# The head of a fused matmul-GELU-matmul kernel: the first two units as plain products, top rows of x first, W1 tile 1 loaded ahead of the bottom rows

## The chip, the cores and the metric

One Trainium2 chip, one core. The metric is the device time of one execution in microseconds (us). A time is quoted as the median of its runs; the state of every run that is compared below is fast, or "unknown" where a kernel was run only once.

Most of the argument is about tenths of a microsecond in a run of 855 us, which times cannot show: single runs of one kernel spread over 2 us and more. So I use a second measure, the **lead**. From the end of unit 2's period on (23.6 us in the first trace of before; units are explained below) both kernels give PE (TensorE, the matmul engine) the same sequence of matmuls, to the last one. The lead of a run at some moment is the start of one such matmul in the first trace of the kernel before, minus the start of the same matmul in that run. "The lead at 40 us" is taken at the matmul that starts at 40.02 us in the trace of before. A positive lead is time won.

## The reference

```python
batch, m, k, h, n = 16, 512, 768, 3072, 768     # x (16,512,768), w1 (768,3072), b1 (3072), w2 (3072,768)

def reference(x, w1, b1, w2):
    y = np.matmul(x, w1) + b1
    y = 0.5 * y * (1.0 + erf(y / np.sqrt(2.0)))
    return np.matmul(y, w2).astype(np.float32)
```

## The kernel before

The 8192 rows of x are worked off in blocks of 1024. The first product is made in units: a unit is one block times 256 columns of W1 (a "W1 tile"). Rows and columns are split in two, and a unit is computed by seven products of half size instead of eight (a Strassen scheme), each product being 3 matmuls of 128x128 weights and 512 columns. The price is sums of operands on VectorE (DVE): four per W1 tile (`prep_wt`) and four per block of x (`x_sums`).

Units overlap. Period n holds products 1, 5, 6, 2 of unit n and products 7, 3, 4 of unit n-1. ScalarE (ACT) copies between banks of PSUM, the memory that PE writes to, and applies GELU; DVE adds. In these traces an engine does not pass over an operation that has to wait (in run h1 below PE stands still for 3.7 us at a product whose weights have not landed, with other products behind it), which is why the place of an operation in the program matters here.

```python
def prep_wt(n):                     # four sums of one W1 tile, 0.36 us each, queued for DVE
    o = {s: w1_op(wts[n], s) for s in range(7)}
    for d, a, b in ((T3, B22, T1), (T1, T1, B11), (T2, B22, T1), (T4, B21, T2)):
        later(KQ * P, lambda d=d, a=a, b=b: tt(o[d], o[a], o[b], SUB), soon)

def period(i, j, fill):             # i: this unit, j: the one before; cut to the order
    p1(i); copy_xy(i)               # PE, then ACT: bank bX -> bank bY
    p7(j); fill(1); p5(i); fill(2); p3(j); fill(3)
    p6(i)                           # PE accumulates into the bank that copy_xy wrote
    j.right_done(); fill(4)         # ACT: GELU of what DVE added after p3
    p4(j); fill(5); p2(i); fill(6)

def fill_a(pos, slot):              # what is done between the products in period pos; cut
    if pos == at[1, 0] - 2 and slot in (2, 5):          # period 5
        transpose_pe(1, X1_PE[slot // 3])               # next x tiles 3 and 7: PE, then an ACT copy
    if slot == (1 if pos < at[1, 0] else 4) and ...:
        prep_wt(seq[pos + 1][1])                        # the next unit's W1 tile
    if slot == 4 and pos == 3:
        prep_wt(0)
    if slot == 1 and pos in (at[1, 0] - 2, at[1, 0] - 1):
        x_sums(1, soon, ...)                            # half of the next block's x sums each
    ...
```

POOL (GpSimd) issues the loads that convert to half precision; in the traces they land in the order of issue (in that of before x tiles 4 to 7 at 10.8 to 13.7 us, W1 tiles 1 to 3 at 15.7, 17.7 and 19.7 us):

```python
for t in range(4, 8): load_x(0, t)       # x tiles 4..7 (the bottom rows)
for n in range(1, 4): load_wt(n)         # W1 tiles 1, 2, 3
# loads_a(0):
load_wt(4); load_next_x(1, (0, 4, 1, 5)); load_wt(5); load_next_x(1, (2, 6, 3, 7)); load_wt(6)
```

x tiles 0 to 3 and W1 tile 0 come in single precision on the queue of SP (SyncE) and are cast on DVE and ACT. The head then runs unit 0 as eight plain products, because there is no time yet for sums. `spin` issues dummy products that are meant to keep PE's clock up (run h1 below shows the clock after an idle stretch):

```python
nc.vector.tensor_copy(out=w1_raw(wts[0])[:, 0:KQ, :], in_=wf[:, 0:KQ, :])
nc.scalar.copy(out=w1_raw(wts[0])[:, KQ:2 * KQ, :], in_=wf[:, KQ:2 * KQ, :])
...
plain(bX[0], 0, 0, 0)
transpose_pe(0, 4)
plain(bX[0], 0, 0, 1)
transpose_pe(0, 5, nc.vector.tensor_copy)
x_sums(0, soon, top, (0, 1)); flush(soon)
transpose_pe(0, 6)
plain(bY[0], 0, 1, 0)
transpose_pe(0, 7)
x_sums(0, soon, bottom, (0, 1)); flush(soon)
plain(bY[0], 0, 1, 1)
spin(2)
... # the bottom rows of unit 0, then prep_wt(1), the other x sums, and units 1, 2, ... in periods
```

Of the kernel before, what the change touches and what calls it, by code (L numbers as in the profile page):

```python
# [10 lines left out]
P = 128  # L11
ADD = mybir.AluOpType.add
SUB = mybir.AluOpType.subtract
GELU = mybir.ActivationFunctionType.Gelu
# [8 lines left out]
def kernel(  # L23
# [8 lines left out]
    nc = tc.nc  # L32
# [5 lines left out]
    RH = SB // 2  # L38
    nsb = R // SB
    KQ = K // P // 2  # L40
# [56 lines left out]
    Gs = [halves(0), halves(GR)]  # L97
# [20 lines left out]
    def w1_raw(wt):  # L118
        return wt[:, 0:4 * KQ * P].rearrange("p (k c) -> p k c", c=2 * P)

    def w1_op(wt, slot):
        raw = wt[:, 0:4 * KQ * P].rearrange("p (a k b c) -> p a b k c", a=2, k=KQ, b=2)
        if slot in RAW:
            return raw[:, RAW[slot][0], RAW[slot][1]]
        return wt[:, slot * KQ * P:(slot + 1) * KQ * P].rearrange("p (k c) -> p k c", c=P)
# [58 lines left out]
    with tc.manual_schedule():  # L184
# [16 lines left out]
        def flush(q):  # L201
            while q:
                q.pop(0)[1]()
# [20 lines left out]
        def prep_wt(n):  # L224
# [3 lines that stand above are left out]
# [59 lines left out]
        def xh_of(sb, t):  # L287
            if sb < ONE:
                return cut(sb * GR + GR // 2 + t * K, K)
            return xh_late[t % 3]  # L290
# [5 lines left out]
        def xT_of(sb, t):  # L296
            return XTs[sb][:, t // NU, :, (t % NU) * P:(t % NU + 1) * P]

        def transpose_dma(sb, t):
            nc.sync.dma_start_transpose(out=xT_of(sb, t), in_=xhs[t])  # L300

        def transpose_pe(sb, t, copy=nc.scalar.copy):
            for kc in range(2 * KQ):
                nc.tensor.transpose(out=bT[t % 2][:, kc, :], in_=xhs[t][:, kc * P:(kc + 1) * P],
                                    identity=ident[:])
            copy(out=xT_of(sb, t), in_=bT[t % 2][:])

        def blocks(sb):
            XT = XTs[sb]
            return [XT[:, a, c:c + KQ, :] for a in range(2) for c in (0, KQ)]  # L310

        def x_sums(sb, q, r=slice(0, RH), ks=range(4)):
            A11, A12, A21, A22 = [a[:, :, r] for a in blocks(sb)]
            S1, S2, S4 = [a[:, :, r] for a in XSs[sb]]
            n = KQ * len(range(RH)[r])
            ops = ((S1, A21, A22, ADD), (S2, S1, A11, SUB), (A21, A11, A21, SUB), (S4, A12, S2, SUB))
            for k in ks:
                later(n, lambda k=k: tt(*ops[k]), q)
# [400 lines left out]
        make_identity(nc, ident[:])  # L719
        make_identity(nc, idf)  # L720
        nc.gpsimd.tensor_copy(out=xh_of(0, 4)[:, 0:1], in_=xf[:, 0, 0:1])
        for t in range(4, 8):
            load_x(0, t)
        for n in range(1, 4):
            load_wt(n)

        def spin(n):

            for k in range(n):
                nc.tensor.matmul(out=(bX[1], bY[1])[k % 2][:], lhsT=zero[:, 0, 0:P], rhs=zero[:, 0, :],  # L730
                                 start=True, stop=True, skip_group_check=True)

        spin(9)
        for t in range(4):
            xhs[t] = xh_of(0, t)
            nc.vector.tensor_copy(out=xhs[t], in_=xf[:, t, :])
            transpose_pe(0, t)
            if t == 0:
                nc.tensor.transpose(out=bW[:, 0:2 * NH], in_=bf, identity=idf[0:2 * NH, 0:2 * NH])
                nc.scalar.copy(out=b1t[:], in_=bW[:, 0:2 * NH])  # L740
            spin(2)
        nc.vector.tensor_copy(out=w1_raw(wts[0])[:, 0:KQ, :], in_=wf[:, 0:KQ, :])
        nc.scalar.copy(out=w1_raw(wts[0])[:, KQ:2 * KQ, :], in_=wf[:, KQ:2 * KQ, :])

        def plain(dst, row, side, half):
            slot = ((B11, T1), (B21, B22))[half][side]
            for c in range(KQ):
                nc.tensor.matmul(out=dst[:, 0:RH], lhsT=w1_op(wts[0], slot)[:, c, :],
                                 rhs=blocks(0)[2 * row + half][:, c, :],
                                 start=half == 0 and c == 0, stop=half == 1 and c == KQ - 1,  # L750
                                 skip_group_check=True)

        def plain_done(dst, row, side):
            nc.scalar.activation(out=Gs[0][side][:, 0, row, :], in_=dst[:, 0:RH], func=GELU,
                                 bias=b1t[:, side:side + 1])

        top, bottom = slice(0, 2 * P), slice(2 * P, RH)
        plain(bX[0], 0, 0, 0)
        transpose_pe(0, 4)
        plain(bX[0], 0, 0, 1)  # L760
        transpose_pe(0, 5, nc.vector.tensor_copy)
        x_sums(0, soon, top, (0, 1))
        flush(soon)
        transpose_pe(0, 6)
        plain(bY[0], 0, 1, 0)
        transpose_pe(0, 7)
        x_sums(0, soon, bottom, (0, 1))
        flush(soon)
        plain(bY[0], 0, 1, 1)
        spin(2)  # L770
        for row, banks in enumerate(((bX[0], bY[0]), (bW, bZ))):
            for side in range(2):
                if row:
                    plain(banks[side], row, side, 0)
                    plain(banks[side], row, side, 1)
                plain_done(banks[side], row, side)
        prep_wt(1)
        last = [soon.pop()]
        for k in (2, 3):
            for r in (top, bottom):  # L780
# [19 lines left out]
        def loads_a(pos):  # L800
            if pos == 0:
                load_wt(4)
                load_next_x(1, (0, 4, 1, 5))
                load_wt(5)
                load_next_x(1, (2, 6, 3, 7))
                load_wt(6)
            for n in range(7, NH):
                if pos == at[1, over[n]] + 1:
                    load_wt(n)
            if pos in w2_at_pos:  # L810
                load_w2(*w2_at_pos[pos])

        X1_PE = (3, 7)

        def fill_a(pos, slot):
            if pos == at[1, 0] - 2 and slot in (2, 5):
                transpose_pe(1, X1_PE[slot // 3])
            if slot == (1 if pos < at[1, 0] else 4) and pos + 1 < len(seq) and seq[pos + 1][0] == 0:
                prep_wt(seq[pos + 1][1])
            if slot == 4:  # L820
                if pos == 3:
                    prep_wt(0)
                for m, c in ((21, 9), (22, 0), (23, 3), (23, 6)):
                    if pos == m:
                        prep_w2(T2, c, queue)
                        prep_w2(T3, c, late if m == 23 else queue)
                if pos == 23:
                    for c in range(0, NH, W2C):
                        prep_w2(T4, c, late)
            if slot == 1:  # L830
                if pos in (at[1, 0] - 2, at[1, 0] - 1):
                    h = pos - at[1, 0] + 2
                    x_sums(1, soon, slice(h * RH // 2, (h + 1) * RH // 2))
                if pos == at[0, NH - 1] + 2:
                    for c in range(0, NH, W2C):
                        prep_w2(T1, c, queue)
                    for k in (0, 1):
                        g_sum(k, 0)
            if pos > at[0, NH - 1]:
                if slot in (1, 4):  # L840
                    sums((0, 1100, 0, 0, 1500)[slot])
            elif slot in (1, 2, 4, 5):
                sums((0, 600, 300, 0, 600, 300)[slot])
            if slot == 5:
                loads_a(pos)
                if 1 <= pos < 5:
                    for t in (pos - 1, pos + 3):
                        if t not in X1_PE:
                            transpose_dma(1, t)
                if seq[pos][0] == 1:  # L850
                    keep(seq[pos][1])
            if slot == 6:
                flush(soon)
# [184 lines left out]
            units += [(Unit3, sb, k) for k in range(7)]  # L1038
        prev = None
        for g, (kind, sb, k) in enumerate(units):  # L1040
            if g == 0:
                loads_a(0)
                continue
            cur = kind(g, sb, k)
            if g < len(seq):
                period(cur, prev, lambda slot: fill_a(g, slot))
            else:
                f = {Unit1: fill_mm1, Unit2: fill_lean if sb else fill_mm2_one, UnitH: fill_hyb,
                     Unit3: fill_mm2_two}[kind]
                period(cur, prev, lambda slot: f(sb, k, slot))  # L1050
            prev = cur
# [30 lines left out]
```

## Time and profile before

| | before |
|---|---|
| time, median of the 3 runs there were | 855.16 us (854.98 to 856.19) |
| span of the profiled run | 854.0 us |
| PE busy | 845.9 us, 99% |
| first useful product | 9.93 us |
| unit 3's first product | 25.1 us |

From the page of the kernel before: each engine's busy time and share of the span, PE's busy tenths in 40 slices of the span, and the chain of waits that ended last.

```profile
PE 845.9 (99%) x6407; PEld 566.5 (66%) x6407; DVE 667.5 (78%) x1128; ACT 423.9 (50%) x688; POOL 83.7 (10%) x135
...
PE   8999999999999999999999999999999999999998
...
PE 96%; DMA 3%; POOL 0%; issue 0%; DVE 0%
```

PE is the limit nearly everywhere; only the first and the last slice have room, and the change is about the first. The timeline of the head shows that room (lines picked out of it). Columns: start, duration, engine, line, operation, output<-inputs and shape, count, and in brackets the idle time of the engine before it with what ended it.

```profile
7.92 0.56 DVE L736 CAST arena<-arena 128x768 f16<-128x768 f32 x1 [0.84 <-DMA arena<-in_x_dram]
9.08 0.80 ACT L306 COPY arena<-bT 128x768 f16<-128x768 f16 x1 [0.45 <-PE bT L304]
9.93 0.81 PE L748 MATMUL bX<-arena 128*128 128x512 f16 x3 [0.46 <-ACT arena L306]
10.96 0.49 PE L304 MATMUL bT<-ident,arena 128*128 128x128 f16 x6 [0.22 <-DMA arena<-in_x_dram]
17.81 0.81 PE L379 MATMUL bX<-arena 128*128 128x512 f16 x3
24.46 1.46 PE L379 MATMUL bX<-arena 128*128 128x512 f16 x6
```

L736 is the cast of x tile 3, L306 the copy of its transpose, L748 the plain products, L304 the transpose of an x tile as it lands, L379 the products of the seven-product units. Between 9.93 and 17.81 us PE has 24 matmuls to do (5.2 us) and four transposes (1.4 us), 6.6 us of work in 7.9. The six matmuls at 24.46 are product 2 of unit 2 and product 1 of unit 3, which starts at 25.1.

L189 is DVE's sums (here the preparation of W1 tile 6), L632 and L395 an addition and the GELU that waits for it, L597 `copy_xy`, and the six matmuls at 41.96 begin with product 6 of unit 6, which needs that copy:

```profile
36.34 1.14 DVE L189 TENSOR_TENSOR arena<-arena 128x384 f16<-128x384 f16 x3
37.39 0.68 DVE L632 TENSOR_TENSOR arena<-bZ,arena 128x512 f32<-128x512 f32 x1
38.11 1.15 ACT L395 ACTIVATE arena<-arena,b1t 128x1024 f16<-128x1024 f32 x1 [0.26 <-DVE arena L632]
40.02 0.81 PE L379 MATMUL bY<-arena 128*128 128x512 f16 x3
41.00 0.60 ACT L597 COPY bY<-bX 128x512 f32<-128x512 f32 x1
41.96 1.46 PE L379 MATMUL bY<-arena 128*128 128x512 f16 x6
```

The copy ends at 41.60 and PE starts at 41.96 without having waited: some 0.3 us are to spare (0.36, less some 0.05 for handing over, as in the trace of after below).

### The profile page before, as it was taken

The numbers are of one execution on the slowest core, as the hardware profiler recorded it, in microseconds if no ns is written. First come the engines' busy times: TensorE is split into PE (matmuls) and PEld (weight loads), VectorE is DVE, ScalarE is ACT, GpSimd is POOL, SyncE is SP. The second block draws the span as 40 slices with busy tenths as digits, with TensorE's granted clock in tenths as the row PEclk, the third lists the DMA queues.
The fourth block names the chain that finished last, engine by engine and source line by source line (L and its number), as shares of the span: only waits on it lengthen the run. The fifth ranks groups of instructions, "written<-read, shape, count | busy, mean of one in ns | idle before, by whom it ended". The sixth has DMA issues, their size and how long they took to land.

```text
span 854.0 us, 16428 instructions
## 1 busy us (share of the span) xinstructions
PE 845.9 (99%) x6407; PEld 566.5 (66%) x6407; DVE 667.5 (78%) x1128; ACT 423.9 (50%) x688; POOL 83.7 (10%) x135
## 2 busy tenths in 40 slices
PE   8999999999999999999999999999999999999998
PEld 4444445687544897448974499645995469944798
DVE  5856678786657998669976799667996689957997
ACT  5777762122277513874138722477216771267611
POOL 5021100002100002000020000200012000010000
PEclk9999999999999999999999999999999999999999
DMA  9996987659989698996989889897998969967397
GB/s 226 235 232 89 256 165 269 240 194 216 234 225 291 212 321 293 265 287 228 333 287 271 254 275 334 274 339 158 313 347 264 307 170 333 348 218 266 101 304 286
DMA packets 143522, 219.05 MB, mean 256 GB/s; under 512 B 61756, under 2 KB 84724, under 8 KB 143444
## 3 DMA queue, kind: packets, MB, share of 16 engines
q1 hardware_dynamic: 117968, 179.83, 65.7%
q0 software_dynamic: 25440, 38.15, 21.1%
q8 instruction: 50, 0.82, 0.4%
q14 instruction: 28, 0.23, 0.1%
q10 hardware_dynamic: 36, 0.01, 0.0%
HBM read 180.30 MB, written 47.87 MB: 267 GB/s over the span
## 4 chain that ended last, share of the span: by engine, by line
PE 96%; DMA 3%; POOL 0%; issue 0%; DVE 0%
PE bY L379 21%; PE bY L484 15%; PE bX L379 14%; PE bX L484 10%; PE bZ L379 7%; PE bW L379 7%; PE bZ L484 5%; PE bW L484 5%; PE bY L423 5%; DMA arena<-w1s 2%; PE bZ L423 2%; PE bX L423 2%; PE bW L423 2%; DMA arena<-in_x_dram 1%; PE bY L571 1%; PE bX L571 1%
## 5 line engine op out<-in xcount | busy, mean ns | idle before, releaser
L189 DVE TENSOR_TENSOR arena<-arena 128x1536 f16<-128x1536 f16 (+7 forms) x632 | 403.5, 669 | 6.5 <-PE bW L423 1.1
L379 PEld LDWEIGHTS <-arena 128*128 128x128 f16 x1995 | 194.2, 98 | 229.6 <-DMA arena<-w1s 3.9
L484 PEld LDWEIGHTS <-arena 128*128 128x128 f16 x3528 | 292.1, 98 | 8.3 <-issue 0.3
L379 PE MATMUL bY<-arena 128*128 128x512 f16 x855 | 216.7, 379 | 0.0
L604 DVE TENSOR_TENSOR arena<-bY,arena 128x512 f32<-128x512 f32 (+1 forms) x103 | 70.1, 680 | 130.1 <-PE bY L379 89.6
L379 PE MATMUL bX<-arena 128*128 128x512 f16 x570 | 140.4, 379 | 1.5 <-DMA arena<-w1s 1.5
L597 ACT COPY bY<-bX 128x512 f32<-128x512 f32 (+1 forms) x144 | 79.2, 550 | 120.7 <-DVE arena L533 87.3
L484 PE MATMUL bY<-arena 128*128 128x192 f16 x1500 | 138.3, 246 | 0.0
L395 ACT ACTIVATE arena<-arena,b1t 128x1024 f16<-128x1024 f32 x95 | 109.2, 1149 | 54.8 <-DVE arena L632 54.8
L617 ACT COPY arena<-bW 128x512 f32<-128x512 f32 (+1 forms) x148 | 81.6, 552 | 91.5 <-PE bW L484 43.5
L484 PE MATMUL bX<-arena 128*128 128x192 f16 x1020 | 93.1, 246 | 0.0
L632 DVE TENSOR_TENSOR arena<-bZ,arena 128x512 f32<-128x512 f32 (+1 forms) x103 | 70.0, 679 | 22.8 <-PE bZ L379 18.8
L379 PE MATMUL bZ<-arena 128*128 128x512 f16 x285 | 77.0, 379 | 0.0
L379 PE MATMUL bW<-arena 128*128 128x512 f16 x285 | 77.0, 379 | 0.0
L423 PEld LDWEIGHTS <-arena 128*128 128x128 f16 x528 | 51.6, 98 | 34.1 <-issue 0.2
L400 ACT ACTIVATE arena<-bX,b1t 128x512 f16<-128x512 f32 x95 | 64.7, 681 | 10.4 <-PE bX L379 10.3
L516 POOL DMA_DIRECT2D out_dram<-arena x42 | 30.6, 728 | 395.1 <-DVE arena L628 358.6
L400 ACT ACTIVATE arena<-bY,b1t 128x512 f16<-128x512 f32 x95 | 64.0, 674 | 0.0
L648 ACT COPY bZ<-bY 128x512 f32<-128x512 f32 (+1 forms) x54 | 29.0, 537 | 65.5 <-DVE arena L632 30.5
L294 POOL DMA_DIRECT2D arena<-in_x_dram x60 | 32.5, 546 | 260.9 <-DMA arena<-arena 152.9
L650 DVE COPY bZ<-bY 128x512 f32<-128x512 f32 (+1 forms) x63 | 43.5, 691 | 6.3 <-DVE arena L632 0.5
L484 PE MATMUL bZ<-arena 128*128 128x192 f16 x504 | 48.5, 246 | 0.0
(60 smaller groups left out, 392.3 us busy)
## 6 DMA issues: line engine op xcount, KB each, us to landing
arena<-w2s SPq DMA_DIRECT2D x294, 288.0 KB, 4.7
arena<-w1s SPq DMA_DIRECT2D x72, 672.0 KB, 6.4
out_dram<-arena POOLq DMA_DIRECT2D x42, 384.0 KB, 5.4
w2s<-arena SPq DMA_DIRECT2D x49, 288.0 KB, 3.1
arena<-in_x_dram POOLq DMA_DIRECT2D x60, 192.0 KB, 6.8
w1s<-arena SPq DMA_DIRECT2D x12, 672.0 KB, 8.1
arena<-in_w_dram POOLq DMA_DIRECT2D x17, 384.0 KB, 8.5
out_dram<-arena SPq DMA_DIRECT2D x17, 384.0 KB, 3.4
```

What stands on the lines that cost most here:

```text
L189: nc.vector.tensor_tensor(out=o, in0=a, in1=b, op=op)
L294: nc.gpsimd.dma_start(out=xhs[t], in_=xr[:, sb * 8 + t, :])
L379: nc.tensor.matmul(out=dst[:, 0:RH], lhsT=w1_op(self.wt, slot)[:, c, :], rhs=a[:, c, :], start=first and c == 0, stop=c == self.C - 1, ski ...
L395: nc.scalar.activation(out=self.G[1][:, hi, :, :], in_=self.tmp, func=GELU, bias=b1t[:, 2 * hi + 1:2 * hi + 2])
L400: nc.scalar.activation(out=self.G[0][:, hi, row, :], in_=bank[:, 0:RH], func=GELU, bias=b1t[:, 2 * hi:2 * hi + 1])
L423: nc.tensor.matmul(out=dst[:, 0:N2], lhsT=a, rhs=w[:, :, c, :], start=first and c == 0, stop=c == self.C - 1, skip_group_check=True)
L484: nc.tensor.matmul(out=dst[:, t * N4:(t + 1) * N4], lhsT=a, rhs=w[:, c, :], start=first and c == 0 and t == ts[0], stop=c == NQ - 1, skip_ ...
L597: nc.scalar.copy(out=bY[u.g % 2][:, 0:u.F], in_=bX[u.g % 2][:, 0:u.F])
L604: nc.vector.tensor_tensor(out=u.c22(), in0=bY[u.g % 2][:, 0:u.F], in1=w[:, 0:u.F], op=ADD)
L617: nc.scalar.copy(out=w[:, 0:u.F], in_=bW[:, 0:u.F])
L632: nc.vector.tensor_tensor(out=u.c12(), in0=bZ[:, 0:u.F], in1=w[:, 0:u.F], op=ADD)
L650: nc.vector.tensor_copy(out=bZ[:, 0:u.F], in_=bY[u.g % 2][:, 0:u.F])
```

## The change

The intent: give PE something to do while the bottom rows of x arrive. Unit 1 becomes a plain unit too, W1 tile 1 is loaded ahead of x tiles 4 to 7, and the top rows of both units are computed first. The remaining bottom rows follow in pieces of 256 columns. The last piece of unit 1 sits inside unit 2's period. The sums of W1 tile 1, which unit 1 no longer needs, are made in period 4 for its use with the next block. The first pieces are made smaller so that PE starts earlier.

```diff
         nc.gpsimd.tensor_copy(out=xh_of(0, 4)[:, 0:1], in_=xf[:, 0, 0:1])
+        load_wt(1)
         for t in range(4, 8):
             load_x(0, t)
-        for n in range(1, 4):
+        for n in range(2, 4):
             load_wt(n)
 ...
-            transpose_pe(0, t)
+            transpose_pe(0, t, copy_halves if t == 3 else nc.scalar.copy)
 ...
-        nc.vector.tensor_copy(out=w1_raw(wts[0])[:, 0:KQ, :], in_=wf[:, 0:KQ, :])
-        nc.scalar.copy(out=w1_raw(wts[0])[:, KQ:2 * KQ, :], in_=wf[:, KQ:2 * KQ, :])
+        for r, c in ((slice(0, KQ), slice(0, P)), (slice(0, KQ), slice(P, 2 * P)),
+                     (slice(KQ, 2 * KQ), slice(0, 2 * P))):
+            nc.vector.tensor_copy(out=w1_raw(wts[0])[:, r, c], in_=wf[:, r, c])
 ... (plain and plain_done take the unit, and a range of rows)
+        for half in range(2):
+            for side in range(2):
+                plain(0, 0, side, half)
+        for side in range(2):
+            plain_done(0, 0, side)
+        plain(1, 0, 0, 0)
         transpose_pe(0, 4)
+        plain(1, 0, 0, 1)
+        plain_done(1, 0, 0)
         transpose_pe(0, 5, nc.vector.tensor_copy)
+        plain(1, 0, 1, 0)
+        transpose_pe(0, 6)
+        plain(1, 0, 1, 1)
+        plain_done(1, 0, 1)
+        plain(0, 1, 0, 0, top)
+        plain(0, 1, 1, 0, top)
+        transpose_pe(0, 7, nc.vector.tensor_copy)
 ... (the other top pieces, the x sums, the bottom pieces; no dummy products)
-        prep_wt(1)
+        prep_wt(2)
 ...
+            if pos == 2 and slot == 1:
+                plain(1, 1, 1, 1, bottom)
+                plain_done(1, 1, 1)
             if slot == 4:
-                if pos == 3:
-                    prep_wt(0)
+                if pos in (3, 4):
+                    prep_wt(pos - 3)
```

More of the change, by code (lines that the diff above doesn't have):

```diff
@@ L300, in transpose_dma, with copy_halves @@
             nc.sync.dma_start_transpose(out=xT_of(sb, t), in_=xhs[t])
+        def copy_halves(out, in_):
+            for c in (slice(0, KQ), slice(KQ, 2 * KQ)):
+                nc.scalar.copy(out=out[:, c, :], in_=in_[:, c, :])
         def transpose_pe(sb, t, copy=nc.scalar.copy):
@@ L741 @@
             spin(2)
-        nc.vector.tensor_copy(out=w1_raw(wts[0])[:, 0:KQ, :], in_=wf[:, 0:KQ, :])
-        nc.scalar.copy(out=w1_raw(wts[0])[:, KQ:2 * KQ, :], in_=wf[:, KQ:2 * KQ, :])
-        def plain(dst, row, side, half):
+        for r, c in ((slice(0, KQ), slice(0, P)), (slice(0, KQ), slice(P, 2 * P)),
+                     (slice(KQ, 2 * KQ), slice(0, 2 * P))):
+            nc.vector.tensor_copy(out=w1_raw(wts[0])[:, r, c], in_=wf[:, r, c])
+        banks = {(0, 0): (bX[0], bY[0]), (1, 0): (bX[1], bY[1]),
+                 (0, 1): (bW, bZ), (1, 1): (bX[1], bY[1])}
@@ L746, in plain @@
+        def plain(n, row, side, half, r=slice(0, RH)):
             slot = ((B11, T1), (B21, B22))[half][side]
             for c in range(KQ):
-                nc.tensor.matmul(out=dst[:, 0:RH], lhsT=w1_op(wts[0], slot)[:, c, :],
-                                 rhs=blocks(0)[2 * row + half][:, c, :],
-                                 start=half == 0 and c == 0, stop=half == 1 and c == KQ - 1,
-                                 skip_group_check=True)
-        def plain_done(dst, row, side):
-            nc.scalar.activation(out=Gs[0][side][:, 0, row, :], in_=dst[:, 0:RH], func=GELU,
-                                 bias=b1t[:, side:side + 1])
@@ L757, with plain_done @@
-        top, bottom = slice(0, 2 * P), slice(2 * P, RH)
-        plain(bX[0], 0, 0, 0)
+                nc.tensor.matmul(out=banks[n, row][side][:, r], lhsT=w1_op(wts[n], slot)[:, c, :],
+                                 rhs=blocks(0)[2 * row + half][:, c, r],
+                                 start=half == 0 and c == 0 and r.start == 0,
+                                 stop=half == 1 and c == KQ - 1, skip_group_check=True)
+        def plain_done(n, row, side):
+            nc.scalar.activation(out=Gs[0][side][:, n, row, :], in_=banks[n, row][side][:, 0:RH],
+                                 func=GELU, bias=b1t[:, 2 * n + side:2 * n + side + 1])
@@ L759 @@
+        top, bottom = slice(0, 2 * P), slice(2 * P, RH)
+        for half in range(2):
[4 more added lines that the diff above has]
+        plain(1, 0, 0, 0)
         transpose_pe(0, 4)
-        plain(bX[0], 0, 0, 1)
+        plain(1, 0, 0, 1)
+        plain_done(1, 0, 0)
         transpose_pe(0, 5, nc.vector.tensor_copy)
+        plain(1, 0, 1, 0)
+        transpose_pe(0, 6)
+        plain(1, 0, 1, 1)
@@ L762 @@
+        plain_done(1, 0, 1)
+        plain(0, 1, 0, 0, top)
+        plain(0, 1, 1, 0, top)
+        transpose_pe(0, 7, nc.vector.tensor_copy)
+        plain(0, 1, 0, 1, top)
+        plain(0, 1, 1, 1, top)
+        for side in range(2):
+            for half in range(2):
+                plain(1, 1, side, half, top)
         x_sums(0, soon, top, (0, 1))
-        flush(soon)
-        transpose_pe(0, 6)
-        plain(bY[0], 0, 1, 0)
-        transpose_pe(0, 7)
         x_sums(0, soon, bottom, (0, 1))
@@ L768 @@
         flush(soon)
-        plain(bY[0], 0, 1, 1)
-        spin(2)
-        for row, banks in enumerate(((bX[0], bY[0]), (bW, bZ))):
-            for side in range(2):
-                if row:
-                    plain(banks[side], row, side, 0)
-                    plain(banks[side], row, side, 1)
-                plain_done(banks[side], row, side)
-        prep_wt(1)
+        for side in range(2):
+            for half in range(2):
+                plain(0, 1, side, half, bottom)
+            plain_done(0, 1, side)
@@ L778 @@
+        plain(1, 1, 0, 0, bottom)
+        plain(1, 1, 0, 1, bottom)
+        plain_done(1, 1, 0)
+        plain(1, 1, 1, 0, bottom)
+        prep_wt(2)
         last = [soon.pop()]
@@ L813, with transposes_a @@
         X1_PE = (3, 7)
+        def transposes_a(pos):
+            for t in (pos - 1, pos + 3):
+                if t not in X1_PE:
+                    transpose_dma(1, t)
         def fill_a(pos, slot):
+            if pos == 2 and slot == 1:
+                plain(1, 1, 1, 1, bottom)
+                plain_done(1, 1, 1)
             if pos == at[1, 0] - 2 and slot in (2, 5):
@@ L845, in fill_a @@
                 loads_a(pos)
-                if 1 <= pos < 5:
-                    for t in (pos - 1, pos + 3):
-                        if t not in X1_PE:
-                            transpose_dma(1, t)
+                if pos < 5:
+                    transposes_a(pos)
                 if seq[pos][0] == 1:
@@ L1040 @@
         for g, (kind, sb, k) in enumerate(units):
-            if g == 0:
-                loads_a(0)
+            if g < 2:
+                loads_a(g)
+                if g:
+                    transposes_a(g)
                 continue
```

## The prediction

> **What bounds it now.** PE: busy 845.9 of 854.0 us (page, part 1), 96% of the chain of waits (part 4). The change touches only the first 25 us; what it saves should survive, as everything later follows PE's pace.
>
> **The head now (timeline).** x tiles 0 to 3 are cast at 4.01, 5.45, 6.40, 7.92 us, the first half of W1 tile 0 at 9.00. The first product starts at 9.93, after waiting 0.5 us for ACT's 0.80 us copy of x tile 3. The chain runs through x tiles 4 to 7, transposed as they land (10.96, 11.94, 12.81, 13.81); unit 0 ends at 17.8, unit 3 starts at about 25.1. From 9.93 to 17.8, 24 matmuls at 0.216 us (six start in 1.29) are 5.2, four transposes of 0.34 are 1.4: about 1.3 us are gaps and dummy products. Another 0.17 is lost at 19.1.
>
> **What the change does.**
> - Unit 1 as 8 plain products instead of 7: three more matmuls, +0.65 us.
> - PE has W1 tile 1 and the top rows to work on while the bottom rows arrive: up to 1.3 us, and the 0.17, can go.
> - x tile 3 is copied in halves (estimate 0.45 us each, from 0.80), W1 tile 0 cast in DVE pieces of about 0.3, 0.3, 0.56 us (0.56 measured for 768 columns): first product at 9.6, -0.3.
> - 36 matmuls of 256 columns replace 18 of 512. The Trainium skill (TensorE: Matmul & The Clock Gate, "Back-to-back issue gap") gives N/2.4 + 2.5 ns, 109 ns; its 216 for 512 agrees with this trace. +0.05, at most +0.2.
> - Loads: same bytes, other order. The Trainium skill (DMA: Bandwidth & Descriptors, "Issuing engines are not separate DMA queues") has all queues on the same 16 engines. Read from when POOL's waits end, a W1 tile takes 2.0 us, an x tile 0.95. Estimate: W1 tile 1 lands at 11.9 instead of 15.9, x tiles 4 to 7 at 12.9, 13.85, 14.8, 15.85; W1 tiles 2 and 3 unchanged (17.9, 20).
>
> **Sum on the chain.** First product 9.6; 15 matmuls to 12.85; tile 4 at about 12.95 (gap 0.1 to 0.4); then 33 matmuls' worth (7.1), transposes (1.4), 0.15 for the small matmuls: both units complete at 21.7, counting the 0.33 us piece inside unit 2's period. Unit 2 needs 2.6 us: unit 3 starts at 24.35 against 25.1. Gain about 0.75 us.
>
> DVE is the risk: x sums start after tile 7's copy (17.6) and end at about 23.2; PE needs the first at 22.1, the last at 25. Preparing tile 1 moves to period 4, so periods 3 and 4 carry about 5.0 us of DVE work in 4.53; I estimate DVE 1.5 us behind, within the 2 us before PE waits.
>
> **Prediction: 854.4 us**, 8 in 10 between 853.6 and 855.4. Faster by over 2%: 0.5%; within: 99%; slower: 0.5%.
>
> **What would show it.** First product near 9.6; W1 tile 1's first near 12.2; tile 4's transpose near 13 after a gap under 0.5; no dummy product after 9.5; unit 3's first product near 24.35; no PE wait on DVE between 21 and 45 us; then 4.53 us periods and a span shorter by 0.75.
>
> **What would make it wrong.** W1 tile 1 landing after 12.5, interleaved with x tile 3 and W1 tile 0, pushing all x tiles. DVE so late that it holds PE. A later DMA wait (W1 rereads near 260 and 372 us) absorbing the shift.

## The result, and the profile after

| | before | after |
|---|---|---|
| time, median | 855.0 us (854.53 to 856.19, 6 runs) | 854.96 us (853.71 to 856.6, 6 runs) |
| span of the profiled run | 854.0 us | 852.4 us |
| first useful product | 9.93 us | 10.02 us |
| unit 3's first product | 25.1 us | 24.4 us |
| lead at 40, 43, 50 us | | 0.73, 0.18, 0.09 us |

The ratio is 0.9999, with a 95% interval of 0.9986 to 1.0012. A ratio is the mean time of one kernel's fast runs over that of the other's of the same rounds, so it is not quite the ratio of the medians above. No change of the time is to be seen. The page of the changed kernel, the same lines:

```profile
PE 845.8 (99%) x6432; PEld 569.2 (67%) x6432; DVE 667.8 (78%) x1128; ACT 421.1 (49%) x686; POOL 83.3 (10%) x135
...
PE   9999999999999999999999999999999999999998
...
PE 93%; DMA 5%; ACT 1%; DVE 0%; issue 0%; POOL 0%; ACTq 0%
```

The head, lines that answer to those of before (L741 is now the cast of x tile 3, L304 the half copies, L757 the plain products, L308 the transposes, L383 the units):

```profile
8.05 0.83 DVE L741 CAST arena<-arena 128x768 f16<-128x768 f32 x1 [0.53 <-DMA arena<-in_x_dram]
9.49 0.86 ACT L304 COPY arena<-bT 128x384 f16<-128x384 f16 x2 [0.56 <-PE bT L308]
10.02 0.81 PE L757 MATMUL bX<-arena 128*128 128x512 f16 x3
...
12.62 0.81 PE L757 MATMUL bX<-arena 128*128 128x512 f16 x3
13.27 0.50 PE L308 MATMUL bT<-ident,arena 128*128 128x128 f16 x6
...
23.73 1.46 PE L383 MATMUL bX<-arena 128*128 128x512 f16 x6
```

From 10.02 us PE works without a gap. W1 tile 1 is there when it is needed (12.62), and x tile 4 as well (13.27). The loads landed as estimated: W1 tile 1 at 12.0 us (11.9 predicted), x tiles 4 to 7 at 13.0, 14.0, 14.9 and 15.8 (12.9 to 15.85), W1 tiles 2 and 3 at 17.8 and 19.9 (17.9 and 20). Six matmuls of 256 columns start in 0.65 us, so one takes the predicted 0.109. Unit 3 starts at 24.4 instead of 25.1, so the lead is 0.73 us, and I had summed it up to 0.75. Twenty microseconds later most of it is gone:

```profile
36.47 1.14 DVE L189 TENSOR_TENSOR arena<-arena 128x384 f16<-128x384 f16 x3 [0.32 <-DMA arena<-in_w_dram]
37.53 0.68 DVE L636 TENSOR_TENSOR arena<-bZ,arena 128x512 f32<-128x512 f32 x1
38.24 1.15 ACT L399 ACTIVATE arena<-arena,b1t 128x1024 f16<-128x1024 f32 x1 [1.12 <-DVE arena L636]
39.29 0.81 PE L383 MATMUL bY<-arena 128*128 128x512 f16 x3
41.13 0.60 ACT L601 COPY bY<-bX 128x512 f32<-128x512 f32 x1
41.78 1.46 PE L383 MATMUL bY<-arena 128*128 128x512 f16 x6 [0.38 <-ACT bY L601]
```

Read it upwards. PE waits at 41.78 for `copy_xy` on ACT. ACT reaches that copy late because its GELU (38.24) waited 1.12 us for DVE's addition (L636). DVE was late because the preparation of W1 tile 6 stands ahead of that addition, and waited 0.32 us for that tile's load. In both kernels this string of work stands at nearly the same absolute time (36.34 and 36.47 us), though PE before it was 0.73 us earlier. The chain of waits of the two kernels up to 46 us says the same. Before, from 12.8 us on it is PE (but for 0.01 us):

```profile
36.27 0.34 PE bT L304 x6
36.61 0.65 PE bZ L379 x3
```

After (start, duration, what), it leaves PE at 41.78 and goes back through ACT and DVE into the stream of loads, and does not come back to PE:

```profile
13.26 11.10 DMA arena<-in_x_dram
24.35 0.28 issue
24.64 11.81 DMA arena<-in_w_dram
36.44 0.02 issue
36.47 0.37 DVE arena L189
...
41.78 1.46 PE bY L383 x6
```

The loads are what did not move. By the traces' packet records POOL's queue starts at 8.7 us in both kernels and keeps step in both, whatever the order: as many bytes as everything up to and including W1 tile 5 makes (3456 KB) are through at 26.9 us before and 27.0 after, and those of all x tiles ahead of W1 tile 6 at 31.5 in both. The last packet of W1 tile 6 is in at 35.6 and 36.0, and its semaphore is complete at 35.99 and 36.44. Run h1 below adds that this landing does not follow PE: there PE was 5 us late, and the tile landed at 35.99.

**A trap.** The profiled spans differ by 1.6 us, and the profiled runs' times by as much (855.75 and 854.13). This is not the change. The lead is 0.09 us from 50 to 255 us, and then jumps: 0.67 at 300, 0.29 at 380, 1.2 at 392 us. The first jump is a delay in the first trace of before itself: all 13 other traces, b2_before's too, gain 0.47 to 0.59 us on it between 255 and 300 us. The jumps lie where PE waits for W1 tiles that are read back (`w1s`). The two traces, and the second trace of the unaltered kernel before (label b2_before, told below), differ there:

```profile
PE bX L379 <- DMA arena<-w1s: 1.5, 3, 1.2
```

```profile
PE bX L383 <- DMA arena<-w1s: 0.5, 1, 0.5
```

```profile
PE bX L379 <- DMA arena<-w1s: 6.7, 4, 2.7
```

That is: total us waited, times, longest, for before, after, and before again. The last of them took 861.33 us with no change at all.

### The profile page after: what moved, and what is told of

Its sections match the earlier page's. It is cut to its first block, busy times and chain, and to the rows that moved or that the text cites. A ratio compares the mean times of both kernels' runs of the same rounds, so it can differ in the third digit from the quotient of the medians.

```text
span 852.4 us, 16481 instructions
## 1 busy us (share of the span) xinstructions
PE 845.8 (99%) x6432; PEld 569.2 (67%) x6432; DVE 667.8 (78%) x1128; ACT 421.1 (49%) x686; POOL 83.3 (10%) x135
## 4 chain that ended last, share of the span: by engine, by line
PE 93%; DMA 5%; ACT 1%; DVE 0%; issue 0%; POOL 0%; ACTq 0%
PE bY L383 20%; PE bY L488 15%; PE bX L383 13%; PE bX L488 10%; PE bZ L383 7%; PE bW L383 7%; PE bZ L488 5%; PE bW L488 5%; PE bY L427 5%; DMA arena<-in_x_dram 3%; PE bZ L427 2%; PE bW L427 2%; PE bX L427 2%; DMA arena<-in_w_dram 1%; DMA arena<-w1s 1%; PE bY L575 1%
## 5 line engine op out<-in xcount | busy, mean ns | idle before, releaser
L383 PEld LDWEIGHTS <-arena 128*128 128x128 f16 x1974 | 192.4, 98 | 225.7 <-DMA arena<-w1s 1.8
L383 PE MATMUL bY<-arena 128*128 128x512 f16 x846 | 214.4, 379 | 0.4 <-ACT bY L601 0.4
L383 PE MATMUL bX<-arena 128*128 128x512 f16 x564 | 138.6, 379 | 0.6 <-DMA arena<-w1s 0.5
L636 DVE TENSOR_TENSOR arena<-bZ,arena 128x512 f32<-128x512 f32 (+1 forms) x102 | 69.3, 679 | 22.7 <-PE bZ L383 18.7
L383 PE MATMUL bZ<-arena 128*128 128x512 f16 x282 | 76.2, 379 | 0.0
L383 PE MATMUL bW<-arena 128*128 128x512 f16 x282 | 76.2, 379 | 0.0
L488 PE MATMUL bW<-arena 128*128 128x192 f16 x504 | 48.5, 246 | 0.0
```

The source lines that it names most:

```text
L383: nc.tensor.matmul(out=dst[:, 0:RH], lhsT=w1_op(self.wt, slot)[:, c, :], rhs=a[:, c, :], start=first and c == 0, stop=c == self.C - 1, ski ...
L488: nc.tensor.matmul(out=dst[:, t * N4:(t + 1) * N4], lhsT=a, rhs=w[:, c, :], start=first and c == 0 and t == ts[0], stop=c == NQ - 1, skip_ ...
L636: nc.vector.tensor_tensor(out=u.c12(), in0=bZ[:, 0:u.F], in1=w[:, 0:u.F], op=ADD)
```

## The experiments

Theory **L** (loads): PE's pace near 42 us hangs on a load that lands at a time fixed by the queue, so an earlier PE only waits longer. Rival **D**: DVE has fallen behind because the change put the preparation of W1 tile 1 into period 4. Rival **A**: ACT's own work is too long there. A further rival is that the loss is chance, as the later jumps are.

All outputs are right. The table collects what the texts below use. "Start" is when DVE begins to prepare W1 tile 6. In the changed kernel PE's product at 41.78 starts 5.31 us after it, and its counterpart in before starts at 41.96; so, if that string of work holds PE, the lead behind it is 41.96 - 5.31 - start = 36.65 - start.

| run | lead at 40 us | start | 36.65 - start | lead at 43 us | lead at 50 us |
|---|---|---|---|---|---|
| after (first trace) | 0.73 | 36.47 | 0.18 | 0.18 | 0.09 |
| n1_after | 0.92 | 36.26 | 0.39 | 0.38 | 0.30 |
| e1_prep1_later | 0.59 | 36.03 | 0.62 | 0.59 | 0.52 |
| e2_w6_early | 0.38 | 36.00 | 0.65 | 0.38 | -0.11 |
| e4_three_dummies | 0.75 | 36.05 | 0.60 | 0.60 | 0.49 |
| h1_w1_behind_x | -5.05 | 41.84 | -5.19 | -5.19 | -5.27 |
| h2_whole_copies | 0.14 | 36.66 | -0.01 | 0.00 | -0.50 |
| e5_pool_later | 1.12 | 36.19 | 0.46 | 0.46 | 0.37 |
| b2_before | -0.14 | 36.63 | 0.02 | -0.14 | -0.14 |
| e6_w6_late | -0.23 | 37.44 | -0.79 | -0.80 | -0.88 |
| v1_prep1_later_keeps | 0.75 | 36.37 | 0.28 | 0.27 | 0.19 |
| e3_x_transposes_early | 1.02 | 36.40 | (chain altered) | 0.41 | -0.18 |
| v5_all | 0.97 | 36.45 | (chain altered) | -0.26 | -0.73 |

In every row that keeps the string of work as it is, the lead at 43 us is the smaller of the lead at 40 us and 36.65 - start, within 0.03 us. The 5.31 comes from the first row, so the other rows test it. They test the string of work, whatever sets its start: DVE waited for tile 6's load before it in after, n1, e1, e5, e6 and v1 (0.20 to 0.70 us; 0.06 in b2), and came to it later than the load in e2, e4, h1 and h2.

### n1_after: the changed kernel again

No edit.

> The changed kernel again, unaltered. In the first pair of traces the same product on PE starts 0.73 us earlier than in the kernel before from about 24 us on (the lead), the lead falls to 0.18 at 42 us and to 0.09 at 46 us, and later moves by up to 1 us at the reloads of W1 near 260 to 390 us. If the fall at 42 us is a property of the schedule, it repeats within 0.1 us; if it is chance like the later ones, the lead at 50 us lands anywhere from 0 to 0.7. Time: within 0.1% of before either way.

Measured: 855.04 us (853.95 to 855.83) against 855.04 us of before, ratio 0.9999 (0.9985 to 1.0014). The lead was 0.92, 0.38 and 0.30 us at 40, 43 and 50 us. The fall repeats (0.54 us against 0.55), so it is not chance. The lead itself varies with the first landings, and widely: the seven runs with the head of the changed kernel (after, n1, e1, e2, e3, e6, v1) have leads of -0.23 to 1.21 us at 30 us. Their median is 0.75.

### b2_before: the kernel before again

No edit.

> The kernel before, again, to see how far its own first 25 us move from run to run. Its leads against its first trace should be within 0.3 us of 0 from 24 to 255 us, with no fall at 42 us; after 260 us they may move by 1 us.

Measured: the lead is -0.14 us all the way from 24 to 255 us. There is no fall at 42 us. After 260 us it loses 5 us to reloads of W1 (the third wait line above), far more than the 1 us I had allowed. So in the head a difference under 0.2 us means nothing (and larger ones between single runs little, see n1), and the reloads decide a single run's time.

### e1_prep1_later: tile 1 prepared in period 7

```diff
-                if pos in (3, 4):
-                    prep_wt(pos - 3)
+                if pos == 3:
+                    prep_wt(0)
 ...
+            if pos == at[1, 0] and slot == 1:
+                prep_wt(1)
```

> The preparation of W1 tile 1 (4 DVE operations, 1.46 us) moved from period 4 to period 7. Theory D (DVE is behind because of this preparation): the lead at 50 us comes back to 0.5 or more. Theory L (DVE waits for W1 tile 6, whose landing did not move): DVE is free earlier but still waits for tile 6 until about 36.4 us, its wait there grows from 0.32 us to over 1 us, and the lead at 50 us stays within 0.1 of 0.09.

Measured: one run, 862.28 us. The lead stayed: 0.59, 0.59, 0.52. Taken alone this speaks for D, and against L as I had put it. But tile 6 happened to be usable at 36.03 us in this run, 0.2 to 0.4 earlier than in the two runs of the changed kernel, and then L too has nothing to take away. The run could not tell them apart. It also had a cost of its own: PE waited 6.2 us for W1 tile 7 near 57 us, because write-backs of W1 tiles, queued behind that of tile 1, had moved to 48 to 54 us and met that load. The rest of the 8.6 us that the lead lost there goes with a granted clock of 0.55 from 60.5 to 66 us.

### v1_prep1_later_keeps: the same without the jam

```diff
 (on top of e1)
-                if seq[pos][0] == 1:
+                if seq[pos][0] == 1 and seq[pos][1] not in range(1, 7):
                     keep(seq[pos][1])
+                if pos == at[1, 1]:
+                    for k in range(2, 7):
+                        keep(k)
 ... (keep(1) just before the loads of period 9)
```

> e1 again (tile 1 prepared in period 7), with the write-backs of W1 tiles 2 to 6 queued ahead of that of tile 1, which waits for its preparation. In e1 they stood behind it, ran 10 us later and met the load of W1 tile 7. Expected: no 6.2 us wait of PE near 57 us; the lead at 43 us is the smaller of the lead at 40 us and 36.65 minus DVE's start on tile 6; at 50 us it is within 0.1 of that and it is still there at 100 us: 0.2 to 0.7.

Measured: one run, 853.75 us; no wait for W1 tile 7; lead 0.75, 0.27, 0.19. This time the tile was late, and DVE, with nothing of tile 1 to do, waited longer for it:

```profile
34.98 0.69 DVE L608 TENSOR_TENSOR arena<-bY,arena 128x512 f32<-128x512 f32 x1 [0.90 <-PE bY L383]
36.37 1.15 DVE L189 TENSOR_TENSOR arena<-arena 128x384 f16<-128x384 f16 x3 [0.70 <-DMA arena<-in_w_dram]
```

DVE was free 0.7 us before tile 6 and PE waited 0.32 us for ACT at 41.69 us: the lead still fell to what the start of that preparation allows. D alone is out as the cause. It keeps a part: in the changed kernel DVE is free only at about 36.1 us (its addition at 35.47 takes 0.68), so even an instant load would have left no more than 36.65 - 36.1, about 0.5 us.

### e6_w6_late: one more load ahead of W1 tile 6

```diff
                 load_next_x(1, (2, 6, 3, 7))
+                nc.gpsimd.dma_start(out=cut(o_w2, K), in_=xr[:, 8, :])
                 load_wt(6)
```

> The changed kernel with one more load of an x tile (192 KB, never read) queued just ahead of W1 tile 6. Theory L in numbers: the lead after 42 us is 36.65 minus the time at which DVE starts to prepare W1 tile 6. The extra load takes 1.0 to 1.4 us there, so DVE starts at 37.3 to 37.7, its wait for the load grows to about 1.5 us, and the lead at 43 us is -0.6 to -1.1, from about 0.8 at 40 us. If the landing is not what holds PE (only the amount of DVE and ACT work is), the lead at 43 us stays at 0.2 to 0.6.

Measured: one run, 857.91 us. DVE started at 37.44 us and the lead at 43 us was -0.80, against -0.79 from the rule. Its wait for the load was 0.33 us and not 1.5, because in this run the head was slow (lead -0.23 at 40 us instead of the 0.8 I had assumed; PE waited 1.3 us for a cast of x) and DVE came later as well. So the run shows that PE follows the start, and the start the landing, but it is a smaller step than intended.

### e4_three_dummies: 0.65 us of PE work added to the head

```diff
         transpose_pe(0, 7, nc.vector.tensor_copy)
 ...
+        spin(3)
         for side in range(2):
             for half in range(2):
                 plain(1, 1, side, half, top)
```

> Three dummy products of 0.216 us added to the head (0.65 us of PE work) behind the top rows of x. If the lead is lost because the work at 36 to 42 us hangs on loads that land at a fixed time (L, and D in so far as it hangs on the landing of x tile 7): the lead at 40 us is 0.08, and at 50 us it is 0.0 to 0.1, so 0.65 us of extra work costs under 0.1 us. If it is lost to something that follows PE's own pace: the lead at 50 us falls to about -0.55.

Measured: one run, 853.97 us; lead 0.75, 0.60, 0.49. The dummies ran (17.19 to 17.84 us), but the first landings were early by chance: the first product started at 9.30 us instead of 10.02. So the lead at 40 us was not 0.08, and the test of "extra work is free" was not made. What stands is that even with the addition the lead at 50 us is 0.49 us, among the largest, which fits a limit set by the loads but does not prove it. No wait for tile 6 was recorded; DVE itself was free only at 36.05.

### e2_w6_early: W1 tile 6 loaded ahead of the next x tiles 3 and 7

```diff
-                load_next_x(1, (2, 6, 3, 7))
-                load_wt(6)
+                load_next_x(1, (2, 6))
+                load_wt(6)
+                load_next_x(1, (3, 7))
```

> W1 tile 6 is loaded ahead of the next x tiles 3 and 7 instead of behind them; nothing else. Theory L: no DVE wait on W1 tile 6 near 36.4 us (0.32 us before), the DVE and ACT work behind it moves up by 0.3, and the lead at 50 us is 0.4 to 0.7. Theory D: the lead at 50 us stays at 0.1 to 0.2. Theory A (ACT is the limit, with the copy of x tile 7 among its work there): 0.1 to 0.2 as well.

Measured: one run, 854.28 us; lead 0.38, 0.38, -0.11. DVE's wait for tile 6 was gone and it started at 36.00, as L says. But the lead did not survive: x tiles 3 and 7 now came late, PE lost 0.4 us at its transpose of tile 3 at 35.7 us, and DVE waited 0.5 us at 39.3 us for x tiles transposed by the DMA engines. The expected 0.4 to 0.7 was wrong: moving one load forward moves others back, and they are needed just as soon.

### e3_x_transposes_early: ACT's copy of x tile 7 out of the way

```diff
-            if pos == at[1, 0] - 2 and slot in (2, 5):
-                transpose_pe(1, X1_PE[slot // 3])
+            if (pos, slot) in ((at[1, 0] - 3, 5), (at[1, 0] - 2, 2)):
+                transpose_pe(1, X1_PE[pos - at[1, 0] + 3])
```

> The two PE transposes of the next x tiles 3 and 7 each one place earlier (end of period 4 and early in period 5), so that ACT's 0.8 us copy of tile 7 no longer stands between its GELU and the copy that PE waits for at 42 us. In four traces that wait ended 5.31 us after DVE began the preparation of W1 tile 6 (36.0 to 36.5 us). If that chain through ACT is what takes the lead away, it becomes 0.5 to 0.8 us shorter, PE does not wait there, and the lead at 50 us is within 0.15 of the lead at 40 us, so 0.6 to 0.9. If DVE alone is the limit, the lead falls at 42 us by 0.4 or more as before. Time: 0.5 us shorter than before at best, under 0.1%, so the interval will hold 1 either way.

Measured: 854.58 us (853.6 to 855.25) against 854.75 of before, ratio 0.9993 (0.9978 to 1.0008). PE no longer waited for ACT. It waited for DVE instead, 0.4 us for its next addition and 0.4 us for its next copy, and the lead went 1.02, 0.41, -0.18:

```profile
36.40 1.15 DVE L189 TENSOR_TENSOR arena<-arena 128x384 f16<-128x384 f16 x3 [0.73 <-DMA arena<-in_w_dram]
39.45 2.09 DVE L189 TENSOR_TENSOR arena<-arena 128x768 f16<-128x768 f16 x4 [0.25 <-DMA arena<-arena]
41.46 0.68 DVE L608 TENSOR_TENSOR arena<-bY,arena 128x512 f32<-128x512 f32 x1
```

Theory A alone is out as the cause: with ACT's part 0.8 us shorter the loss was larger, as the next wait, on DVE (0.38 us), stood just behind it. DVE waits for loads twice here (tile 6, then the DMA transposes), and its queue behind them is full.

### h1_w1_behind_x: the old order of loads

```diff
-        load_wt(1)
         for t in range(4, 8):
             load_x(0, t)
-        for n in range(2, 4):
+        for n in range(1, 4):
```

> The changed kernel with the old order of loads: W1 tile 1 behind x tiles 4 to 7. The products of unit 1 then stand in PE's order ahead of x tile 4 but their weights land near 15.5 us. Expected: PE waits about 2.5 to 3 us from about 12.6 us, unit 3's first product about 2 us later than in the changed kernel, lead at 40 us between -1 and -2. If the order of loads did not matter, the lead would stay at 0.7 to 0.9.

Measured: one run, 859.46 us; lead -5.05 at 40 us, so the new order of work needs the new order of loads. W1 tile 6 landed at 35.99 us all the same, as in the trace of before. The loss is three times what I expected, and the wait itself is only 3.7 us of it. The rest is the clock: from the end of the wait to 21.38 us half pace costs some 2.9 us (the first product had come 1.0 us earlier than in the changed kernel's first trace). Columns: stretch, its length, busy us and instructions of PE, PEld, DVE, ACT and POOL, the granted clock, the DMA share, GB/s:

```profile
12.00:15.50 3.50, 0.00 (x0) 0.00 (x0) 0.00 (x0) 0.60 (x2) 1.49 (x3) 0.86 1.38 195
15.50:21.50 6.00, 5.94 (x28) 3.41 (x29) 0.56 (x1) 1.49 (x2) 1.91 (x3) 0.51 1.42 200
```

After the wait PE ran at 0.51 of its clock for 6 us. The Trainium skill (TensorE: Matmul & The Clock Gate, "What's actually happening") gives half clock after an idle window of about 3.4 us. The half clock agrees, the time roughly: by the trace's clock records it begins at 14.55 us, 2.7 us after PE fell idle, and in e1 at 61.09 us, 4.0 us after. This is what the dummy products in the head are for.

### h2_whole_copies: without the small pieces

```diff
-            transpose_pe(0, t, copy_halves if t == 3 else nc.scalar.copy)
+            transpose_pe(0, t)
 ... (W1 tile 0 cast in two halves, on DVE and ACT, as before)
```

> The changed kernel with x tile 3 copied whole by ACT and W1 tile 0 cast in two halves on DVE and ACT, as before. If the small pieces bring the first product forward as I predicted, it starts 0.3 us later against x tile 3's cast, and the second half of W1 tile 0 comes from ACT after the copy, so PE waits another 0.2 to 0.5 for it; lead at 40 us 0.2 to 0.5. If the lead comes from the order of the work alone (x tile 4's landing at 12.7 is the limit and not the first product), it stays at 0.7 to 0.9.

Measured: one run, 856.64 us; lead 0.14 at 40 us. The first product came 2.35 us after x tile 3's cast began, against 1.97 in the changed kernel's first trace: 0.38 us. PE did not wait for ACT's half of W1 tile 0. The head was also late by 0.2 us for another reason (that cast began at 8.27 us instead of 8.05), and the cast itself took 0.90 us instead of 0.83. From the end of the cast to the first product it is 1.45 us here and in both traces of before, and 1.13 in that of the changed kernel (1.13 to 1.14 in all its other variants but e4, with 1.25). So the small pieces bring the first product 0.3 us forward, as predicted.

### e5_pool_later: POOL idle while DVE casts

```diff
-        for n in range(2, 4):
-            load_wt(n)
 ... (after the casts of W1 tile 0:)
+        nc.gpsimd.tensor_copy(out=w1_raw(slots[2])[:, 0, 0:1],
+                              in_=w1_raw(wts[0])[:, 2 * KQ - 1, 2 * P - 1:2 * P])
+        for n in range(2, 4):
+            load_wt(n)
```

> POOL issues the loads of W1 tiles 2, 3 and 4 only after the last cast of W1 tile 0, so it is idle from about 7.6 us. If POOL's issuing is what stretches DVE's casts (0.83 us instead of 0.56 for x tile 3, 0.41 to 0.86 for the pieces of 384 columns), the cast of x tile 3 and all three of W1 tile 0 run at one speed here (0.56, 0.43, 0.43 or less, 0.56), and the first product starts 0.2 us sooner after x tile 3's cast begins. If the casts stay uneven, the cause is another. W1 tile 2 lands at 17.1 us as before.

Measured: one run, 852.97 us. The cast of x tile 3 took 0.56 us and the casts of W1 tile 0 0.43, 0.41 and 0.56; in the changed kernel they took 0.83, 0.43, 0.86 and 0.56. The first product came 1.70 us after x tile 3's cast began instead of 1.97. That gain can't be credited to the edit: POOL was still issuing (until 8.31 us) when x tile 3 was cast at 7.63, and in e2, e3 and v1, with POOL unaltered, this cast took 0.56 us as well and the first product came after 1.69 to 1.70. What the edit shows is the casts of W1 tile 0: they are even here and in v5, which has the same edit, and uneven in all but one (e1) of the changed kernel's other runs with small pieces, h1 included (up to 1.01 us). The Trainium skill (SBUF — State Buffer, "Who interferes with whom") has DVE casts in a two-port mode and POOL share one pair of memory ports that only one of them holds at a time; the even casts here agree. The lead was 1.12 at 30 us and fell to 0.46 at 43 us, where the rule puts it.

### v5_all: everything together

```diff
 (e5, e3 and v1's order of write-backs, tile 1 prepared in slot 4 of period 7, and:)
-                if pos in (at[1, 0] - 2, at[1, 0] - 1):
-                    h = pos - at[1, 0] + 2
-                    x_sums(1, soon, slice(h * RH // 2, (h + 1) * RH // 2))
+            x_at = {(at[1, 0] - 2, 4): 0, (at[1, 0] - 1, 1): 1, (at[1, 0] - 1, 4): 2, (at[1, 0], 1): 3}
+            if (pos, slot) in x_at:
+                for r in (top, bottom):
+                    x_sums(1, soon, r, (x_at[pos, slot],))
```

> A version made from the findings: the changed kernel with POOL issuing W1 tiles 2 to 4 later (e5), tile 1 prepared in period 7 with the write-backs reordered (v1), the PE transposes of the next x tiles 3 and 7 one place earlier (e3), and the eight x sums of the second block spread one kind at a time over periods 5 to 7 instead of standing in DVE's queue behind W1 tile 6. W1 tile 6 still lands at about 36.0 to 36.4 us, but less work hangs on it before PE needs it: ACT's part is 0.8 us shorter, and DVE has 2 sums instead of 4 ahead of the addition that PE waits for next. Theory L with both chains shortened predicts a lead of 0.9 to 1.2 us at 40 us and at least 0.7 at 50 and 100 us. If some other fixed landing (the DMA transposes, about 39.3 us) takes over, the lead at 50 us is under 0.5. Time: 0.5 to 1 us below the kernel before, about 0.1%, which five rounds will hardly separate from nothing.

Measured: 854.14 us (853.86 to 855.57) against 854.84 of before, ratio 0.9993 (0.998 to 1.0007), so no proven gain. The lead of 0.97 at 40 us turned into -0.73 at 50 us. The other outcome named in the expectation happened:

```profile
39.51 0.56 DVE L189 TENSOR_TENSOR arena<-arena 128x768 f16<-128x768 f16 x1 [0.26 <-DMA arena<-arena]
41.66 0.56 DVE L189 TENSOR_TENSOR arena<-arena 128x768 f16<-128x768 f16 x1 [1.59 <-DMA arena<-arena]
```

By taking the first sum of the bottom half early, I made DVE wait 1.59 us for the last DMA transposes, which land at about 41.6 us. They are a second landing behind the first, but not a fixed one: by the semaphores the last of the six transposes landed at 39.7 us in the trace of before, at 41.5 in that of after, and anywhere from 39.0 (h1) to 41.9 (e2) in the others. In the kernels before and after, DVE comes to those sums at 41.65 and 41.79 us, 2.0 and 0.3 us after their data. No version of mine beats the others beyond doubt.

## Why the prediction was right or wrong

The number was right: 854.4 us predicted with 853.6 to 855.4, and 854.96 measured, class "within 2%". It was right partly for the wrong reason, and by luck in so far as the stated range also holds 855.0, the time of the kernel before: it could not tell a gain from none, and the spread of single runs would have hidden a lead of 0.75 us as well.

- **The head, right.** The lead of 0.75 us up to unit 3 was measured as 0.73 and 0.92 us in two runs. In the first trace PE has no gap after its first product, W1 tile 1 was used from 12.62 us (12.2 predicted), x tile 4 transposed at 13.27 (13), unit 3 began at 24.4 (24.35).
- **The first product, wrong.** It was predicted at 9.6 us and came at 10.02 and 9.44 in two runs. In the first trace it starts 0.05 us after ACT's copy of the first half of x tile 3 (9.49 to 9.97), so the delay came through that tile: its cast began at 8.05 us instead of 7.92 and took 0.83 us instead of 0.56, and the half copy took 0.48 instead of 0.45, together 0.43 us. The term "W1 tile 0 cast in DVE pieces of about 0.3, 0.3, 0.56 us" was mis-sized too, but cost nothing there (the first piece was ready at 9.62): undisturbed the pieces take 0.43, 0.41 and 0.56 (e5), and beside POOL's issuing up to 0.86. I had simply halved the 0.56; the Trainium skill (VectorE: DVE Perf Modes, "The TRN2 errata") names a fixed cost per instruction, and these times agree that halving the columns does not halve the cast. That the sum came out right all the same is luck in part: x tile 4's transpose was 0.3 us later than in my sum (13.27 against 12.95), and the rest up to unit 3 took 11.1 us instead of 11.4.
- **"What it saves should survive, as everything later follows PE's pace": the step that failed.** For 0.5 to 0.6 us it did not survive 42 us. What stands there follows the stream of loads, not PE. That stream is a fixed amount of bytes in a queue that is never idle until W1 tile 6 has landed, and the change only reorders it. Before, PE was the slower of the two by about 0.3 us, so the limit was there but unseen; an earlier PE could win only that, and what an earlier landing adds (with a landing at 35.99 us, as in the trace of before, DVE could start at 36.02: by the rule of the table 0.6, as an estimate).
- **"No PE wait on DVE between 21 and 45 us", wrong in the same step.** PE waited 0.38 us at 41.8 us, on ACT, which waited on DVE, which waited on the load. I had estimated DVE to be 1.5 us behind, "within the 2 us before PE waits". The estimate left out that DVE's queue also holds waits for loads, and that ACT stands between DVE and PE.
- **"A span shorter by 0.75", wrong.** The lead that remains at 50 us is 0.09 and 0.30 us, against 0 and -0.14 in two traces of before: a gain of about 0.3 us if one averages two runs each, 0.03% of the time. The profiled span was 1.6 us shorter by chance.
- **"A later DMA wait (W1 rereads near 260 and 372 us) absorbing the shift" was named as a danger and is not what happened.** The shift was gone before. These waits do dominate the spread from run to run.

Open: why the landing of W1 tile 6 varies by 0.4 to 0.6 us between runs (by the packet records of the four traces of the two unaltered kernels it is the last of the sixteen completion writes that varies: fifteen came by 35.0 to 35.1 us in each, the last at 35.57 and 36.18 before, 36.01 and 35.85 after); and whether 0.65 us of extra work in the head is really free, as e4 was spoilt by an early landing. How much of the small second fall (0.07 to 0.11 us between 43 and 50 us where nothing was altered there) has which cause was not tested.

## What to carry to other kernels

Before crediting a saving upstream to the end of the run, look for the next place downstream that hangs on something with its own clock (a queue of loads that is never idle), and read how much slack the limiting engine has there: a saving survives only up to that slack. Follow what an engine waits for through all engines in between; here PE waited for ACT, ACT for DVE, and DVE for a load issued 12 us before. Where single runs spread more than the effect, compare the start of the same instruction in two traces at several points, and repeat the unaltered kernel before believing a difference of spans.

## What the Trainium skill lacked or had wrong

- DMA: Bandwidth & Descriptors gives no figure for a load that runs beside DMA transposes. By the packet records of the changed kernel, POOL's queue moved about 200 KB in a microsecond from 10 to 28 us and 121 KB from 32 to 34 us, while W1 tile 6 was loaded. SP issued six DMA transposes from 23.45 to 38.1 us. No run here took the transposes away, so this is a coincidence in time and not a shown cause.
- The same page has no figure for how far apart the 16 engines can end one load. In the trace of the changed kernel, 15 of the 16 completion writes of W1 tile 6 came by 35.1 us and the last at 36.0.
- SBUF — State Buffer says that whichever of the two starts first holds the shared ports for its whole instruction. In the kernel before, DVE's casts at 7.92 and 9.00 us took 0.56 us each although POOL was issuing loads from 7.19 to 10.78 us, and the issue that had begun at 8.88 took 1.09 us instead of 0.83 to 0.88; in the changed kernel casts beside such issues took 0.83 and 0.86 us. So an issue under way does not always hold up a cast, and the page doesn't say when it does.
